# Rotary half-swaps by DMA, a third place for softmax weights, merged weight buffers, and another start, in a two-layer fp32 trunk on one core

## The chip, the core and the metric

The kernel runs on one core of a Trainium2 chip. The core has a matmul engine (TensorE, PE, with its weight loads listed as PEld), a vector engine (DVE), a scalar engine (ACT), a general engine (POOL) and an engine that only issues DMAs (SP). The metric is the device time of one execution in microseconds.

## The reference

Two layers over 512 positions of width 1024. Every layer does a mixer and a SwiGLU with width 2816, each between a pre-norm and a post-norm. The first mixer is sliding-window attention with 16 query heads, 4 key heads, rotary positions and a learned sink; the second is a gated unit that mixes positions in chunks of 128.

```python
for i in range(DEPTH):                       # 2
    h = rmsnorm(x, norm_mix_pre[i])
    m = swa_sink_attention(h, ...) if i % 2 == 0 else chunked_sgu(h, ...)
    x = x + rmsnorm(m, norm_mix_post[i])
    h = rmsnorm(x, norm_ffn_pre[i])
    x = x + rmsnorm(swiglu(h, ...), norm_ffn_post[i])

# rotary, in the attention, on q and k (after their bias)
x1, x2 = x[..., :half], x[..., half:]
concatenate([x1 * cos - x2 * sin, x2 * cos + x1 * sin])
# per head: window of 128 keys back, softmax with the sink in max and sum
m = maximum(max(s), sink); p = exp(s - m)
probs = p / (sum(p) + exp(sink - m)); o = probs @ v; out = o @ w_o + b_o
```

## The kernel before, in words

**Products.** Every fp32 product is done as three matmuls of a rounded type: high x high, high x low and low x high (`mm3`, line 272). The normed activations are kept as `hh` and `hl`, the weights as `wh` and `wl`. Weights stream from memory in chunks of 128 x 1024 (512 KB, tile `raw`), by DMAs on SP (`fetch`, L303). `split` makes `wh` on ACT (L344) and `wl` on DVE (L325), for the first two chunks on POOL (`POOL_LOW`, L322). The FFN's products need sums or differences of two chunks (L337). There are 4 buffers for `raw` and 15 of the same size for `wh`, `wl` and rows of gains.

**Order.** The order of the instructions on PE, DVE and ACT is written by the Python program itself: it keeps a planned time for each engine (`now`, `busy`), runs PE's work as the main thread, and lets side generators (`Side`, with a due time) put their DVE and ACT instructions in between. SP and POOL execute in the order in which the program issues; SP waits at an issue for a free buffer and for a free one of 8 rotating completion semaphores. Numbers such as `WARM`, `X_0` and `hold` are planned times, and so set where things stand and not how long they take.

**Start.** 26 matmuls on zeros (L240) run while x transposed (`xg`) and weights load; `c_cols` with the gains comes by a DMA on POOL. `start` makes `hh` on ACT (L1390) and `hl` on DVE (L1393). Then the V projection: 64 matmuls with `wh`, 32 with `wl`.

**Attention.** Ten tiles of the Q/K projection (2 groups of 1 key and 4 query tiles) run on PE, 24 matmuls each. `evac_qk` takes each out of PSUM: DVE multiplies with the norm's factor (L960); ACT copies four blocks of 32 partitions, each to its neighbour's place and with its bias, which is the half-swap of the rotary (L966); DVE does the three rotary operations (L969, L971, L972); ACT and DVE split the result in high and low (L976, L979; tiles `ga`, `gb`). Then eight softmax units (2 groups x 4 query blocks): scores on PE with mask and maximum on DVE (L1048), exponentials on ACT (L1070), division (L1079 on DVE, L1083 on ACT); transposes on PE (L1116), which ACT copies to `t` (L1120); P·V on PE (L1108); the output split on ACT (L1130) and DVE (L1135) into `ga`. A unit keeps its weights in one of two `p` tiles, so a unit's scores wait until the unit two before is done (`all_scores`). The output projection (WO) has 8 tiles of 12 matmuls per group, and DVE adds them into the tiles `m` (L1195, L1210); the second group's tiles go by token block (0 to 3, 128 positions each), two column halves each.

**Norms.** When a block's second half is added, the post-norm's chain of small DVE operations (L482 to L471) and the update of `x` (L617) follow. For blocks 0 and 1 together the next pre-norm comes next: another chain, a scaling (L514 or L523), transposes on PE (L552, L554), `hh` on ACT and `hl` on DVE (L571), for which the next product waits. The first FFN ends with blocks 0 and 1 interleaved matmul group by matmul group in both column halves, then block 2, then block 3 (L901).

Of the kernel before, what the change touches and what calls it, by code (L numbers as in the profile page):

```python
# [13 lines left out]
P = 128  # L14
D = 1024
S = 512
# [8 lines left out]
NW = 15  # L25
NP = 2
PITCH = 0.107
NY = 3
P0 = 3
NT = 3  # L30
NRAW = 4
# [7 lines left out]
X_0 = 4.0  # L39
# [5 lines left out]
POOL_LOW = (0, 1)  # L45
ALT = (1, 2, 3)
WARM = 5.5
ORDER = (0, "w", 1, 2, "w", 3)
# [101 lines left out]
def trunk_kernel(ctx, tc, x_t, xt, w, cols, rows, ws_t, consts, out):  # L150
# [7 lines left out]
    rawp = pool("rawp", NRAW)  # L158
# [127 lines left out]
    used, cur, hold, pace = [0], [0], [0.0], [5.1]  # L286
    left = [CB * u for _, _, u in STREAM]
    raw_used = [0]

    def fetch(free=0.0, most=NBLK):  # L290
        while len(raws) < min(NCH, most) and raw_used[0] + len(STREAM[len(raws)][0]) <= NRAW:
            c = len(raws)
            if c == NLATE:
                load_x()
# [6 lines left out]
            for b in reversed(STREAM[c][0]):  # L301
                raw = rawp.tile([P, CB * P], F32, tag="raw", name=nm("raw"))
# [6 lines left out]
    def split():  # L309
        c = len(chunks)  # L310
        fetch()
        tiles, ready = raws[c]
        raw = tiles[0]
        assert used[0] + 2 <= NW
# [34 lines left out]
    def split_idle():  # L349
        c = len(chunks)  # L350
        if c >= NCH or used[0] + 2 + spare[0] > NW or (c and not chunks[c - 1][2].done):
            return False
# [10 lines left out]
    spare, stage = [0], [0]  # L363

    def chunk(i):
        c = i // CB
        while c >= len(chunks):
            until(lambda: not chunks or chunks[len(chunks) - 1][2].done)
            split()
        return c, chunks[c]  # L370
# [19 lines left out]
    def row_tile(o):  # L390
        used[0] += 1
        assert used[0] <= NW
# [17 lines left out]
    c_cols = cp.tile([P, 42], F32, name="c_cols")  # L410
# [32 lines left out]
    def gain(v, k):  # L443
        return c_cols[:, v * KT + k:v * KT + k + 1]

# [258 lines left out]
    def ffn(base, nx_in, g1o, nx_out):  # L704
# [188 lines left out]
        if 1:  # L893
            spare[0] = 0
# [41 lines left out]
    def attention(nx_in, g1o, nx_out):  # L936
# [6 lines left out]
        ready = {}  # L943

        def evac_qk(pr, j, ps, hf):
# [10 lines left out]
            def rest(f):  # L956
# [7 lines left out]
                for q in range(4):  # L964
                    o = (q ^ 1) * 32
                    nc.scalar.activation(ro[o:o + 32, hf], t1[q * 32:q * 32 + 32, hf], AF.Identity, bias=b[q * 32:q * 32 + 32])  # L966
                    f = A(n, f, 0.14)
# [3 lines left out]
                nc.vector.tensor_tensor(ro[:, hf], ro[:, hf], sin[:, hf], ALU.mult)  # L971
# [10 lines left out]
                for t in range(hf.start // P, hf.stop // P):  # L982
                    ready[pr, j, t] = f

# [39 lines left out]
        def scores(u):  # L1024
# [6 lines left out]
            pt = u.pt = ptile()[:].rearrange("p g (i k) -> p g i k", i=2)  # L1031
            for g2 in range(2):
# [12 lines left out]
                for g in range(2):  # L1045
                    for i in range(2):
                        j = (2 * g2 + g) * 2 + i
                        nc.vector.tensor_tensor_reduce(  # L1048
                            pt[:, 2 * g2 + g, i, 0:nk], sc[i][:, g * 256:g * 256 + nk], mask[:, 256 - nk:256], 0.125,
# [12 lines left out]
        def softmax(u, g2, st, es, sm, f):  # L1062
# [3 lines left out]
            p = lambda j: u.pt[:, j // 2, j % 2, 0:u.nk]  # L1066
# [20 lines left out]
        def values(u):  # L1087
# [25 lines left out]
            for z, (i, kt) in enumerate(groups):  # L1113
                pT = aux()
                for g in range(4):
                    nc.tensor.transpose(pT[:, g * P:(g + 1) * P], u.pt[:, g, i, kt * P:(kt + 1) * P], ident)  # L1116
# [35 lines left out]

        def all_scores():
            for i, u in enumerate(order):
                while i >= NP and not order[i - NP].done:
# [3 lines left out]
        def all_values():  # L1159
            for u in order:  # L1160
                yield from values(u)
                u.done = True

# [19 lines left out]
        m = new_m()  # L1183
        stage[0] = 1
        bo = row_tile(3)
        for c, t in ([(c, t) for c in range(2) for t in range(NB)],
# [3 lines left out]
            if 1:  # L1190
                grab("acc")
                ps = acc()
                for k in range(4):
                    tok_mm(ps, osrc(0), t, k, WO0 + 16 * c + 4 * k, k == 0, k == 3)
                nc.vector.tensor_tensor(m[t][c][:], ps[:], bo[:, cols2[c]], ALU.add)  # L1195
# [255 lines left out]
def _layout(inputs):  # L1451
# [58 lines left out]
    vecs += [a["attn_b_qkv"][0][order]]  # L1510
# [36 lines left out]
```

## Time and profile before

| | us |
|---|---|
| median of 3 runs (1058.65 to 1059.26) | 1058.82 |
| the profiled execution | 1059.33 |
| its span | 1057.5 |
| PE busy | 1031.1 (97%) |
| DVE busy | 684.7 (65%) |
| ACT busy | 469.6 (44%) |
| start of the Q/K projection | 23.67 |
| start of the first FFN | 191.43 |
| second FFN's matmuls end near | 1049 |

The stages follow one another on PE: start and V to 23.7, Q/K to 88.8, softmax with WO to 191.4, first FFN to about 546, the gated unit, the second FFN to the end. In a row of the timeline stand start, duration, engine, line, operation, output and inputs, and in brackets the idle time before it with what ended it. A group's row has busy time, mean ns of one, and the idle time before. "Busy" of PE contains modelled ends of pipelined matmuls.

### The profile page before, as it was taken

How to read it: one execution, taken by the hardware profiler on the slowest of the kernel's cores; microseconds unless marked ns; L12 is line 12 of the kernel's file. 1: busy time of each engine (PE TensorE's matmuls, PEld its weight loads, DVE VectorE, ACT ScalarE, POOL GpSimd, SP SyncE). 2: the span in 40 equal slices, each digit the busy share in tenths (PEclk: the TensorE clock that was granted, in tenths of full speed). 3: DMA queues.
4: the chain of work that ended last, by engine and by line, in shares of the span. 5: the costliest groups of instructions: out<-in, count | busy, mean ns of one | idle time of the engine just before them, and what ended most of it. 6: DMA issues, size and time to landing. Idle time of an engine off the chain costs nothing.

```text
span 1057.5 us, 13471 instructions
## 1 busy us (share of the span) xinstructions
PE 1031.1 (97%) x5126; PEld 854.7 (81%) x5126; DVE 684.7 (65%) x1276; ACT 469.6 (44%) x817; POOL 23.8 (2%) x22
## 2 busy tenths in 40 slices
PE   8998998999999999999989999999999999999996
PEld 7875665998888888888878888899888888888885
DVE  6798678743446566778495777474245666687736
ACT  5798666542233343435265343464224333334411
POOL 2000002000000000000010000010000000000000
PEclk9998999999999999999999999999999999999999
DMA  9422011343425644655431333133344553565402
GB/s 334 138 82 80 21 60 41 100 127 113 139 82 178 199 122 157 222 188 191 156 116 60 104 103 121 56 121 120 120 140 131 178 174 124 188 203 193 163 21 80
DMA packets 39057, 138.66 MB, mean 131 GB/s; under 512 B 4368, under 2 KB 4896, under 8 KB 38992
## 3 DMA queue, kind: packets, MB, share of 16 engines
q1 hardware_dynamic: 38304, 136.66, 39.3%
q8 instruction: 40, 0.66, 0.3%
q10 hardware_dynamic: 576, 0.92, 0.2%
q0 software_dynamic: 112, 0.23, 0.2%
q14 instruction: 25, 0.20, 0.1%
HBM read 135.69 MB, written 2.10 MB: 130 GB/s over the span
## 4 chain that ended last, share of the span: by engine, by line
PE 92%; DVE 3%; ACT 2%; issue 1%; DMA 0%; POOL 0%; DVEq 0%; ACTq 0%; POOLq 0%
PE acc L272 89%; PE acc L1108 1%; PE aux L1116 1%; PE aux L554 1%; ACT p L1070 1%; DMA c_cols<-cols 0%; ACT rt L966 0%; DVE wl L325 0%; DVE x L617 0%; DVE hl L1393 0%; ACT wh L344 0%; PE aux L552 0%; ACT t L1120 0%; DVE m L1210 0%; DVE rc L471 0%
## 5 line engine op out<-in xcount | busy, mean ns | idle before, releaser
L272 PE MATMUL acc<-hh,wh 128*128 128x512 f32 (+1 forms) x960 | 352.1, 367 | 0.0
L272 PE MATMUL acc<-hl,wh 128*128 128x512 f32 (+1 forms) x960 | 349.9, 364 | 0.0
L272 PE MATMUL acc<-hh,wl 128*128 128x512 f32 (+1 forms) x960 | 349.7, 364 | 0.0
L325 DVE TENSOR_TENSOR wl<-raw,wh 128x1024 fp32r<-128x1024 f32 x198 | 241.9, 1230 | 151.1 <-PE acc L272 78.2
L272 PEld LDWEIGHTS acc<-hh,wh 128*128 128x128 f32 x960 | 181.1, 189 | 29.4 <-issue 0.2
L272 PEld LDWEIGHTS acc<-hh,wl 128*128 128x128 f32 x960 | 181.1, 189 | 28.7
L272 PEld LDWEIGHTS acc<-hl,wh 128*128 128x128 f32 x960 | 181.1, 189 | 28.6 <-issue 0.2
L344 ACT ACTIVATE wh<-raw 128x1024 fp32r<-128x1024 f32 x160 | 165.6, 1052 | 55.0 <-PE acc L272 48.3
L272 PE MATMUL acc<-wh,rt 128*128 128x512 f32 x496 | 162.3, 389 | 0.0
L272 PE MATMUL acc<-wh,ga 128*128 128x512 f32 (+1 forms) x344 | 120.3, 399 | 3.6 <-DVE ga L1135 2.9
L272 PEld LDWEIGHTS acc<-wh,rt 128*128 128x128 f32 x496 | 93.1, 188 | 19.4
L272 PE MATMUL acc<-wl,rt 128*128 128x512 f32 x248 | 96.5, 389 | 0.0
L272 PEld LDWEIGHTS acc<-wh,ga 128*128 128x128 f32 x344 | 65.2, 191 | 21.1 <-DVE ga L1135 3.8
L853 DVE TENSOR_TENSOR m<-m,acc 128x512 f32<-128x512 f32 x80 | 51.8, 684 | 44.2 <-PE acc L272 33.0
L272 PE MATMUL acc<-wl,ga 128*128 128x512 f32 (+1 forms) x206 | 80.0, 388 | 0.0
L332 ACT ACTIVATE wh<-raw 128x1024 fp32r<-128x1024 f32 x40 | 42.3, 1059 | 71.0 <-DVE raw L337 71.0
L831 ACT ACTIVATE rt<-t 128x512 fp32r<-128x512 f32 x40 | 25.3, 633 | 87.1 <-DVE t L826 68.7
L740 ACT ACTIVATE t<-acc 128x512 f32<-128x512 f32 (+1 forms) x38 | 20.1, 529 | 95.0 <-PE acc L272 95.0
L272 PEld LDWEIGHTS acc<-wl,rt 128*128 128x128 f32 x248 | 46.6, 188 | 9.6
L337 DVE TENSOR_TENSOR raw<-raw,raw 128x1024 f32<-128x1024 f32 x40 | 48.8, 1219 | 0.0
L272 PEld LDWEIGHTS acc<-wl,ga 128*128 128x128 f32 x206 | 39.3, 191 | 6.6
L598 POOL TENSOR_TENSOR m<-m,row 128x512 f32<-128x512 f32 x12 | 16.8, 1407 | 1012.1 <-ACT acc L476 1012.1
(135 smaller groups left out, 990.5 us busy)
## 6 DMA issues: line engine op xcount, KB each, us to landing
raw<-w SPq DMA_DIRECT2D x240, 512.0 KB, 3.6
row<-rows SPq DMA_DIRECT2D x8, 512.0 KB, 5.2
xg<-xt SPq DMA_DIRECT2D x4, 512.0 KB, 7.1
x<-x_t SPq DMA_DIRECT2D x4, 512.0 KB, 11.9
out<-x SPq DMA_DIRECT2D x4, 256.0 KB, 2.1
out<-x ACTq DMA_DIRECT2D x3, 256.0 KB, 2.1
cs<-consts SPq DMA_DIRECT2D x1, 512.0 KB, 8.3
t<-ws_t SPq DMA_DIRECT2D x2, 256.0 KB, 5.9
```

The costliest lines, as they stand in the source:

```text
L272: nc.tensor.matmul(ps, a, b, start=start, stop=stop)
L325: nc.vector.tensor_tensor(wl[:], raw[:], wh[:].bitcast(F32), ALU.subtract)
L332: nc.scalar.activation(wh[:], raw[:], AF.Copy)
L337: nc.vector.tensor_tensor(raw[:], raw[:], tiles[1][:], op)
L344: nc.scalar.activation(wh[:], raw[:], AF.Copy)
L554: nc.tensor.transpose(dst, self.src[t][k // 4][:, (k % 4) * P:(k % 4 + 1) * P], ident)
L598: nc.gpsimd.tensor_tensor(self.m[c][:], self.m[c][:], self.g1[:, cols2[c]], ALU.mult)
L740: nc.scalar.activation(t1[:, hf], pg[:, hf], AF.Silu)
L831: nc.scalar.activation(hi, src, AF.Copy)
L853: nc.vector.tensor_tensor(d, d, ps[i][:], ALU.subtract if sign == "-" else ALU.add)
L1070: nc.scalar.activation(p(j), p(j), AF.Exp, bias=st[:, j:j + 1], accum_out=sm[:, j:j + 1])
L1108: nc.tensor.matmul(po[i * 64:i * 64 + 64, :], vt[n - nkt + 1 + kt][:, o:o + 64], todo[2 * kt + i], start=kt == 0, stop=kt == nkt - 1)
```

## The change

**Half-swaps.** The four ACT copies of a Q/K tile become four DMAs of 32 x 512 (64 KB) on SP, from one tile of a pair to the other. A DMA adds no bias, so ten columns with the swapped bias join `c_cols` (42 to 52) and DVE adds it in the instruction that multiplies with the sine. The planner counts `ROT` = 4.0 us for them.

**Places for softmax weights.** Beside the two `p` tiles a unit can take four `m` tiles, as long as no `m` is in use by WO, or two pairs of rotary tiles once all ten tiles are rotated. `m` tiles are now taken one by one as WO needs them. In the order that the program writes, the `m` place is never taken and the rotary place once, by unit 5 (counted from 0).

**Buffers.** `raw` comes out of the same 19 buffers as `wh` and `wl`; at most 2 are `raw`, 4 in the two stages that need pairs of chunks.

**Start.** Weights are issued before x transposed; `c_cols` comes on ACT's queue, with a first activation that has ACT's table loaded; both first `wl` go to DVE; 37 instead of 26 matmuls on zeros.

**FFN ends.** Block 0's second half is finished before block 1's begins.

```diff
-NW = 15
+NW = 19
+ROT = 4.0
-NRAW = 4
+NRAW = (2, 4)
-X_0 = 4.0
+X_0 = 4.9
-POOL_LOW = (0, 1)
+POOL_LOW = ()
-WARM = 5.5
-ORDER = (0, "w", 1, 2, "w", 3)
+WARM = 8.0
+ORDER = ("w", 0, 1, 2, "w", 3)
...
-                now[0] += 0.214 if now[0] < 4.0 else 0.107
+                now[0] += 0.214
...
-        while len(raws) < min(NCH, most) and raw_used[0] + len(STREAM[len(raws)][0]) <= NRAW:
+        while len(raws) < min(NCH, most):
             c = len(raws)
+            n = len(STREAM[c][0])
+            if raw_used[0] + n > NRAW[stage[0] in (2, 6)] or used[0] + raw_used[0] + n > NW:
+                return
...
-                raw = rawp.tile([P, CB * P], F32, tag="raw", name=nm("raw"))
+                raw = wp.tile([P, CB * P], F32, tag="w", name=nm("raw"))
...
+    nc.scalar.dma_start(c_cols[:], cols)
+    first_act = sp.tile([P, 8], F32, tag="first", name="first", bufs=1)
+    nc.vector.memset(first_act[:], 0.0)
+    nc.scalar.activation(first_act[:], first_act[:], AF.Copy)
     nc.gpsimd.dma_start(c_id[:], consts[:, 1280:1408])
-    nc.gpsimd.dma_start(c_cols[:], cols)
...
-            ends = [(0, 0), (0, 1), (1, 0), (1, 1)]
+            ends = [((0, 1), 0), ((0,), 1), ((1,), 1), ((2,), 0), ((2,), 1), ((3,), 0), ((3,), 1)]
...
-            ends = [((0, 1), 0), ((0, 1), 1)] + [((2 + i,), c) for i, c in ends]
...
-                    hold[0] = now[0] + 4 * BJ * 0.65
+                    hold[0] = now[0] + 5 * BJ * 0.65
...
                 for q in range(4):
                     o = (q ^ 1) * 32
-                    nc.scalar.activation(ro[o:o + 32, hf], t1[q * 32:q * 32 + 32, hf], AF.Identity, bias=b[q * 32:q * 32 + 32])
-                    f = A(n, f, 0.14)
+                    nc.sync.dma_start(ro[o:o + 32, hf], t1[q * 32:q * 32 + 32, hf])
+                f += ROT
...
-                nc.vector.tensor_tensor(ro[:, hf], ro[:, hf], sin[:, hf], ALU.mult)
+                nc.vector.scalar_tensor_tensor(ro[:, hf], ro[:, hf], b_rot(i), sin[:, hf], ALU.add, ALU.mult)
...
+        homes = {"p": NP, "m": 4, "rt": 0}
+        def home(u):
+            if homes["p"]:
+                homes["p"] -= 1
+                u.home = "p"
+            elif len(todo_m) == 8 and homes["m"] == 4:
+                homes["m"] = 0
+                u.home = "m"
+            elif len(rotated) == 10 and slots["rt"] >= 2:
+                slots["rt"] -= 2
+                u.home = "rt"
+            else:
+                return False
+            return True
+
         def all_scores():
             for i, u in enumerate(order):
-                while i >= NP and not order[i - NP].done:
+                while not home(u):
                     yield now[0] + 0.2
                 yield from scores(u)
```

**Three places of the order.** The first is the Q/K projection on ACT, the middle of its first tiles, as it was before (`rt` are the rotary tiles):

```order
L344 ACTIVATE wh_389<-raw_190 128x1024
L344 ACTIVATE wh_404<-raw_237 128x1024
L966 ACTIVATE rt_398<-rt_398,c_cols 32x512 x4
L344 ACTIVATE wh_420<-raw_274 128x1024
L344 ACTIVATE wh_450<-raw_374 128x1024
L976 ACTIVATE gb_119<-rt_398 128x512
L966 ACTIVATE rt_441<-rt_441,c_cols 32x512 x4
L344 ACTIVATE wh_492<-raw_396 128x1024
L976 ACTIVATE ga_117<-rt_441 128x512
L966 ACTIVATE rt_483<-rt_483,c_cols 32x512 x4
```

and SP's issues in the changed kernel over the same tiles:

```order
L307 DMA raw_377<-w 128x1024
L307 DMA raw_408<-w 128x1024
L307 DMA raw_431<-w 128x1024
L978 DMA rt_402<-rt_402 32x512 x4
L978 DMA rt_445<-rt_445 32x512 x4
L307 DMA raw_462<-w 128x1024
L307 DMA raw_482<-w 128x1024
L307 DMA raw_523<-w 128x1024
L978 DMA rt_493<-rt_493 32x512 x4
L307 DMA raw_536<-w 128x1024
L978 DMA rt_538<-rt_538 32x512 x4
L978 DMA rt_574<-rt_574 32x512 x3
```

The half-swaps leave ACT's order and stand between the weight loads on SP, where only loads stood; the third tile's swaps stand behind three loads.

The second is DVE near the end of the attention: the last output split (`ga`, with the accumulator of the last P·V), the adds of WO tiles (`m`) and the updates of `x`. Before:

```order
L617 SCALAR_TENSOR_TENSOR x_91<-m_1013,rc_1826,x_91 128x512
L617 SCALAR_TENSOR_TENSOR x_91<-m_1014,rc_1826,x_91 128x512
L325 TENSOR_TENSOR wl_1838<-raw_1276,wh_1837 128x1024
L1210 TENSOR_TENSOR m_1016<-acc_1804,m_1016 128x512
L1135 TENSOR_TENSOR ga_118<-acc_1782,ga_117 128x4x128
```

and now:

```order
L630 SCALAR_TENSOR_TENSOR x_87<-m_1046,rc_1792,x_87 128x512
L630 SCALAR_TENSOR_TENSOR x_87<-m_1263,rc_1792,x_87 128x512
L1254 TENSOR_TENSOR m_1209<-acc_1754,m_1209 128x512
L1155 TENSOR_TENSOR ga_118<-acc_1713,ga_117 128x4x128
L1254 TENSOR_TENSOR m_1345<-acc_1804,m_1345 128x512
L1254 TENSOR_TENSOR m_1449<-acc_1821,m_1449 128x512
L328 TENSOR_TENSOR wl_1835<-raw_1750,wh_1834 128x1024
```

The last split stood behind block 1's update of `x` (`x_91`) and now stands ahead of block 1's chain, with only block 0's update (`x_87`) before it; two WO tiles are added behind it in these rows and three more later, where two followed before.

The third is DVE at the end of the first FFN. Before:

```order
L901 TENSOR_TENSOR m_2822<-acc_4485,m_2822 128x512
L901 TENSOR_TENSOR m_2824<-acc_4486,m_2824 128x512
L604 TENSOR_TENSOR m_2822<-m_2822,row_4479 128x512
L604 TENSOR_TENSOR m_2824<-m_2824,row_4479 128x512
L901 TENSOR_TENSOR m_2823<-acc_4528,m_2823 128x512
L901 TENSOR_TENSOR m_2825<-acc_4529,m_2825 128x512
L604 TENSOR_TENSOR m_2823<-m_2823,row_4479 128x512
L604 TENSOR_TENSOR m_2825<-m_2825,row_4479 128x512
```

and now:

```order
L913 TENSOR_TENSOR m_2843<-acc_4497,m_2843 128x512
L913 TENSOR_TENSOR m_2845<-acc_4498,m_2845 128x512
L617 TENSOR_TENSOR m_2843<-m_2843,row_4491 128x512
L617 TENSOR_TENSOR m_2845<-m_2845,row_4491 128x512
L913 TENSOR_TENSOR m_2844<-acc_4538,m_2844 128x512
L617 TENSOR_TENSOR m_2844<-m_2844,row_4491 128x512
L495 SCALAR_TENSOR_TENSOR u_4574<-sq_4493 128x1
```

Both blocks' second halves were added and given their gains before block 0's chain began (`u`, in the row behind the last); now block 0's chain starts after its own, and block 1's second half comes later.

More of the change, by code (lines that the diff above doesn't have):

```diff
@@ L286, in trunk_kernel @@
     used, cur, hold, pace = [0], [0], [0.0], [5.1]
+    stage = [0]
     left = [CB * u for _, _, u in STREAM]
@@ L350, in split_idle @@
         c = len(chunks)
-        if c >= NCH or used[0] + 2 + spare[0] > NW or (c and not chunks[c - 1][2].done):
+        if c >= NCH or used[0] + raw_used[0] + 2 > NW or (c and not chunks[c - 1][2].done):
             return False
@@ L361, in split_idle, with room @@
         return True
-    spare, stage = [0], [0]
+    def room():
+        fetch()
+        return len(chunks) in raws and used[0] + raw_used[0] + 2 <= NW
     def chunk(i):
@@ L367, in chunk @@
         while c >= len(chunks):
-            until(lambda: not chunks or chunks[len(chunks) - 1][2].done)
-            split()
+            until(lambda: c < len(chunks) or (not chunks or chunks[len(chunks) - 1][2].done) and room())
+            if c >= len(chunks):
+                split()
         return c, chunks[c]
@@ L390, in row_tile @@
     def row_tile(o):
+        until(lambda: used[0] + raw_used[0] < NW)
         used[0] += 1
-        assert used[0] <= NW
         t = wp.tile([P, D], F32, tag="w", name=nm("row"))
@@ L409, in trunk_kernel @@
     xs = [xp.tile([P, D], F32, tag=f"x{k}", name=f"x{k}") for k in range(NB)]
-    c_cols = cp.tile([P, 42], F32, name="c_cols")
+    c_cols = cp.tile([P, 52], F32, name="c_cols")
     c_msk = cp.tile([P, 384], F32, name="c_msk")
@@ L444, in gain, with b_rot @@
         return c_cols[:, v * KT + k:v * KT + k + 1]
+    def b_rot(i):
+        return c_cols[:, 42 + i:43 + i]
     def b_qk(i):
@@ L943, in attention @@
         ready = {}
+        rotated, todo_m = [], list(range(8))
         def evac_qk(pr, j, ps, hf):
@@ L1030, in scores @@
             st, es, sm = small(8, "st"), small(8, "es"), small(8, "sm")
-            pt = u.pt = ptile()[:].rearrange("p g (i k) -> p g i k", i=2)
+            if u.home == "m":
+                ms = [mp.tile([P, S], F32, tag="m", name=nm("pm"))[:] for _ in range(4)]
+            elif u.home == "rt":
+                ms = [x for _ in range(2) for x in pair()]
+            else:
+                t = ptile()
+                ms = [t[:, g] for g in range(4)]
+            u.pt = [t.rearrange("p (i k) -> p i k", i=2) for t in ms]
             for g2 in range(2):
@@ L1115, in values @@
                 for g in range(4):
-                    nc.tensor.transpose(pT[:, g * P:(g + 1) * P], u.pt[:, g, i, kt * P:(kt + 1) * P], ident)
+                    nc.tensor.transpose(pT[:, g * P:(g + 1) * P], u.pt[g][:, i, kt * P:(kt + 1) * P], ident)
                     now[0] += 0.11
@@ L1181, in attention @@
                 evac_qk(pr, j, proj_tile((Q0, Q1)[pr] + j * KT, KT, h, full), full)
-        m = new_m()
+        m = [[None, None] for _ in range(NB)]
         stage[0] = 1
@@ L1194, in attention @@
                     tok_mm(ps, osrc(0), t, k, WO0 + 16 * c + 4 * k, k == 0, k == 3)
+                until(lambda: homes["m"] + 3 >= 8 - len(todo_m) + 1 or homes["m"] == 4 and len(rotated) == 10)
+                todo_m.pop()
+                m[t][c] = mp.tile([P, S], F32, tag="m", name=nm("m"))
                 nc.vector.tensor_tensor(m[t][c][:], ps[:], bo[:, cols2[c]], ALU.add)
```

18 lines of the change are left out of this document (11 added, 7 removed).

## The prediction

> **What bounds the kernel now.** I read the shares of the engines first, then what the tensor engine (PE) waited for, then the windows by stage.
>
> ```profile
> PE 1031.1 (97%) x5126; PEld 854.7 (81%) x5126; DVE 684.7 (65%) x1276; ACT 469.6 (44%) x817; POOL 23.8 (2%) x22
> ```
> ```profile
> PE acc L1108 <- ACT t L1120: 6.6, 3, 3.8
> PE acc L272 <- ACT wh L344: 3.1, 1, 3.1
> PE acc L272 <- DVE ga L1135: 2.9, 2, 2.6
> PE acc L272 <- DVE hl L571: 2.7, 1, 2.7
> ```
>
> PE is busy 97% of the span and its work does not change, so a gain can only come from places where PE stands or runs at a reduced clock. The waits (us in total, times, longest) are four: the start (`wh` L344), the softmax (`t` L1120, `ga` L1135), and the norm behind the first FFN (`hl` L571). The windows show the stages around the attention; their columns are PE, PEld, DVE, ACT and POOL busy, granted clock, DMA share, GB/s.
>
> ```profile
> 55.00:88.80 33.80, 33.80 (x196) 26.23 (x195) 32.88 (x106) 32.56 (x84) 0.00 (x0) 1.00 0.29 95
> 88.80:107.80 19.00, 14.94 (x67) 7.99 (x66) 14.38 (x35) 15.17 (x33) 0.00 (x0) 0.82 0.17 55
> 107.80:146.00 38.20, 38.20 (x228) 27.42 (x227) 27.80 (x113) 23.14 (x77) 0.00 (x0) 1.00 0.13 42
> 146.00:191.40 45.40, 38.64 (x183) 25.65 (x182) 34.94 (x108) 28.12 (x76) 5.36 (x4) 0.92 0.15 47
> ```
>
> The Q/K projection ends near 88.8 and the first FFN begins near 191.4. Between them PE idles 4.1 us in the second row and 6.8 us in the fourth, and the clock falls there too. How much is lost in all I get from counts and paces. The first list holds PE's matmuls of 88.8 to 191.4, the second pieces of the chain of waits (start, duration, line, count) in which PE never stopped:
>
> ```profile
> L272 PE MATMUL acc<-wh,ga 128*128 128x512 f32 x128 | 48.3, 425 | 3.6 <-DVE ga L1135 2.9 <-ACT ga L1130 0.7
> L272 PE MATMUL acc<-wl,ga 128*128 128x512 f32 x64 | 26.0, 406 | 0.0
> L1108 PE MATMUL acc<-t,vt 128*64 128x512 f32 x52 | 19.1, 636 | 6.6 <-ACT t L1120 6.6
> L1116 PE MATMUL aux<-c_id,p 128*128 128x128 f32 x94 | 15.8, 298 | 0.5 <-ACT t L1120 0.5
> L272 PE MATMUL acc<-gb,ga 64*128 64x256 f32 x96 | 9.2, 331 | 0.0
> L552 PE MATMUL aux<-rt,x 128*128 128x128 f32 x16 | 2.1, 275 | 0.0
> L272 PE MATMUL acc<-gb,ga 64*128 64x128 f32 x24 | 1.8, 281 | 0.0
> ```
> ```profile
> 519.78 17.24 PE acc L272 x76
> 122.63 1.01 PE acc L1108 x4
> 106.91 0.91 PE acc L272 x12
> 188.62 0.89 PE aux L552 x8
> ```
>
> The paces are 17.24/76 = 0.227 us for a 512-wide matmul, 1.01/4 = 0.25 for P·V, 0.91/12 = 0.076 for a score matmul and 0.89/8 = 0.11 for a transpose. The work is 192 x 0.227 + 52 x 0.25 + 120 x 0.076 + 110 x 0.11 = 43.6 + 13.0 + 9.1 + 12.1 = 77.8 us of 102.6. So **24.8 us are lost**, and by the windows nearly all of it before 107.8 and after 146; split as idle plus lost clock stand there (7.5 against 10.4) that is about 10 and 14.
>
> **The start: gain 3.4.**
>
> ```profile
> 7.20 1.33 ACT L1390 ACTIVATE hh<-xg,c_cols 128x512 fp32r<-128x512 f32 x2 [1.07 <-DMA c_cols<-cols]
> 11.84 1.04 ACT L344 ACTIVATE wh<-raw 128x1024 fp32r<-128x1024 f32 x1
> 9.53 0.58 PE L272 MATMUL acc<-wh,hh 128*128 128x256 f32 x1 [3.08 <-ACT wh L344]
> 9.50:12.70 3.20, 3.17 (x15) 3.17 (x16) 2.57 (x2) 3.20 (x5) 2.37 (x1) 0.50 1.02 419
> 16.01 0.39 PE L272 MATMUL acc<-wh,hl 128*128 128x256 f32 x1 [0.84 <-DVE hl L1393]
> 13.07 2.89 DVE hl L1393
> 22.23 1.60 PE L272 MATMUL acc<-wl,hh 128*128 128x256 f32 x12
> 23.67 0.40 PE L272 MATMUL acc<-hh,wh 128*128 128x512 f32 x1
> ```
>
> PE idles 3.08 us before its first real matmul at 9.53, then runs at clock 0.50, then waits 0.84 us for an `hl` that took 2.89 us on DVE while POOL wrote a `wl`. The 12 `wl` matmuls from 22.23 to 23.67 pace at 0.12. Now weights land first, the constants come on ACT's queue, the warm matmuls (37 instead of 26) last until the real ones, and both `wl` are DVE's. What then ends last is the second weight chunk: it is fifth in the queue as before, and its `wh` ended by 12.9 (third number: 11.84 + 1.04). Behind it stand 32 matmuls with `wh` and 32 with `wl`: 64 x 0.12 = 7.7, so Q/K starts near 20.3 instead of 23.67. Bounds: 96 matmuls at 0.12 from an unimproved 9.53 end at 21.1, and with clock 0.50 for 3.2 us at 22.7, so 1.0 at least; 4.5 if the chunk lands 1 us sooner. I take 3.4, the row's own landing.
>
> **The Q/K projection: nothing, and the way into softmax: gain 2.**
>
> ```profile
> L966 ACT ACTIVATE rt<-rt,c_cols 32x512 f32<-32x512 f32 x32 | 23.1, 721 | 3.4 <-DVE rt L960 3.0
> out<-x SPq DMA_DIRECT2D x4, 256.0 KB, 2.1
> 10.46 0.33 SPq L303 DMA_DIRECT2D raw<-w  x1
> ```
>
> The first row is from the list of 27 to 88.8; the other 8 of the 40 half-swaps run after it. The change takes 40 ACT operations of 721 ns (28.8 us) away and adds 40 DMAs of 64 KB on SP, whose rows here are a store with its time from issue to landing and one issue. DVE keeps its operations (the bias moves into an instruction that is there already) and was busy 32.88 of 33.80 us from 55 to 88.8, against 32.56 for ACT: with ACT relieved, DVE still sets the pace, so I cost this edit at nothing in that stage. A tile's four halves took 4 x 0.72 = 2.9 us on ACT. The swap DMA is in no row; the nearest is the 256 KB store, 2.1 us from issue to landing, and with three earlier issues of 0.33 us the fourth lands after some 3.1 us (an estimate from these two rows). That is level with ACT; DVE has other tiles' work to fill it. From below, the swaps cost nothing; from above, each lands behind two weight loads, which the rivals price. After 88.8, PE's longest wait for `t`, 3.8 us, ended while ACT, busy 15.17 of 19.0 us, worked through those last eight halves (8 x 0.72 = 5.8 us) between the exponentials. Not all of that comes back: the last two tiles' DVE operations stay, and so do the exponentials, which the next unit's transposes wait for. I take 2 of the 10 us, a third of the 5.8, with bounds of 0 (DVE ends last there too) and 5.8.
>
> **From there to the FFN: gain 6.** Weights of unit 5 go to two idle rotary tiles; the `m` place is never taken in the written order. With ACT free, the last P·V now stands five WO tiles before the norm instead of before the last two. Then the wait for `ga` (2.6 us) goes, because that split is no longer queued on DVE behind the chains of blocks 0 and 1, and the wait for `t` in this stage (6.6 - 3.8 = 2.8, or less) should go, because the exponentials before it no longer share ACT with late work. But a new wait follows. Its durations are in these DVE rows of the first FFN's end:
>
> ```profile
> 537.65 1.32 DVE L482 SCALAR_TENSOR_TENSOR u<-s 128x1 f32<-128x1 f32 x2
> 539.98 0.23 DVE L471 SCALAR_TENSOR_TENSOR rc<-vw,vz 128x1 f32<-128x1 f32 x2
> 547.47 1.41 DVE L617 SCALAR_TENSOR_TENSOR x<-m,rc,x 128x512 f32<-128x512 f32 x2
> 548.80 0.68 DVE L901 TENSOR_TENSOR m<-acc,m 128x512 f32<-128x512 f32 x1
> 549.40 1.21 DVE L325 TENSOR_TENSOR wl<-raw,wh 128x1024 fp32r<-128x1024 f32 x1
> 550.54 0.87 DVE L571 SCALAR_TENSOR_TENSOR hl<-aux,c_cols,hh 128x256 fp32r<-128x256 f32 x2
> ```
>
> Once token block 1's last WO tile is added, DVE has four more adds (2.7), two `wl` (2.4), block 1's own chain with its `x` (1.2 + 1.4), the joint norm (539.98 + 0.23 - 537.65 = 2.6), its scaling (estimate 0.4) and block 2's chain and `x` (2.6) before the first `hl` (0.4): 13.7, and about one more where it waits for ACT's squares. PE has four WO tiles for it (48 x 0.227 = 10.9) and eight transposes (0.9). So PE stands about 3 us, runs on at half clock for some 3 us (lost: 1.7), and waits some 2 more for the fourth pair of `hl`, which stands behind block 3's chain. That makes 7 of new loss, with 1 in the middle, where 14 were lost: gain 6. Bounds: 12 if the walk's losses shrink to 2, and 0 if the softmax chain of the last units still ends as late.
>
> What the clock does after such a gap is read from two windows:
>
> ```profile
> 153.00:156.00 3.00, 3.00 (x18) 2.68 (x19) 1.89 (x8) 0.97 (x2) 0.00 (x0) 0.50 0.52 171
> 552.00:555.00 3.00, 3.00 (x10) 2.33 (x9) 3.00 (x6) 1.78 (x3) 0.00 (x0) 0.52 0.85 270
> ```
>
> They follow the softmax's second wait for `t` (6.6 - 3.8 = 2.8 us at most) and the 2.7 us wait for `hl`. The Trainium skill ("TensorE: Matmul & The Clock Gate", "HAM oscillation") rules that only idle gaps over about 3.4 us are to be avoided. By that rule a gap of 3 us would cost no clock and this part would gain 1.7 more; the rows show the clock at half after 2.8 and 2.7, so the trace does not agree, and I keep the 1.7.
>
> **The end of the first FFN: gain 4.** PE's 2.7 us wait for `hl` (L571) and the 0.52 clock behind it (0.48 x 3 = 1.4) are 4.1. Block 0's second half is now finished one tile (18 matmuls, 4.1 us) before block 1's, so the joint norm no longer has both chains behind each other ahead of it, and block 1's is one tile further from the transposes. Bounds: 0, if `hl` still stands behind block 2's chain, and 4.5. The second FFN's end keeps its chain; extra raw buffers meet no wait in the trace there: nothing.
>
> **Sum.** 3.4 + 2 + 6 + 4 = 15.4. The profiled execution took 1059.33 (span 1057.5 and 1.8 around it), so 1043.9 by it; the median of the runs before is 0.5 lower. I predict **1044**, with 1034 to 1054 for this case alone.
>
> **Rivals.**
> (1) The attention gains nothing: DVE was as full as ACT, and the relieved engine was never the one that ended last. For it: 32.88 of 33.80. Against it: after 146 DVE has a quarter idle. Only 3.4 and 4 stay: 1052.
> (2) Slower: the swaps come late. SP issues in order; a swap behind a weight load that waits for a free buffer stands with it, and in three of ten tiles the four swaps are split by such loads. What waits behind a late swap on DVE is the next tile's reading of its accumulator, and PE waits for that accumulator; DVE has 0.9 us idle in 33.8, so a late swap lengthens the projection almost directly. At 3 us for each of ten tiles it costs 30, of which I let a third be hidden behind other work; the attention's gains are lost with it: 1059.3 - 7.4 + 20 = 1072. It decides from 2.3 us a tile on, where 10 x 2.3 x 2/3 eats the 15.4. Against it: DMA share is 0.29 in that window. The Trainium skill ("DMA: Bandwidth & Descriptors", "Rules for kernel authors") says that small transfers under 64 KB are mostly overhead and that transfers on disjoint partition parts serialize; by it four in a row would take longer than one after the other issued, which is this rival's side. No row here shows four small transfers together.
> (3) The gap ahead of the norm stays too short to cost the clock, and the softmax chains close up: 1.7 of clock and about 4 of the 8 us that I left on the way into softmax are not lost, 1044 - 5.7 = 1038. This is also where the rule on the clock above leads. For it: ACT is free between the projection and the exponentials. Against it: the two clock rows, and DVE's unchanged work.
> (4) The third place itself does nothing, being used once; this is inside (1) and inside my 6, not priced again.
>
> **Chances.** Forecast 0.58; (1) 0.19; (2) 0.12; (3) 0.11. A measurement of this kernel tells 0.2% (2.1 us) from no change. Of (1), a third may end within it, if the start or the FFN end fails as well. Faster 0.58 + 0.11 + 0.13 = 0.82, same 0.06, slower 0.12. The range leaves out (2) and the low tail of (3): 1033 to 1058.
>
> **What would show it.** Right: first real matmul before 9, Q/K from about 20; no ACT half-swaps, DVE without waits over 1 us for `rt` before 88; last P·V more than 10 us before the FFN; a PE wait for `hl` of 2 to 4 us there; none near the first FFN's end. Wrong: DVE idle behind swap DMAs, PE waiting on `wh` in the projection, or the waits of `t` and `ga` of the same length as before.

## The result, and the profile after

The change takes 1045.34 us (median; 1044.23 to 1047.61) against 1059.04 (1058.65 to 1059.56) on the same chip: ratio 0.9873, 95% interval 0.9855 to 0.9891. The profiled execution took 1044.61 us, its span is 1042.8.

The engines' line, and PE's list of waits, of the changed kernel:

```profile
PE 1023.1 (98%) x5137; PEld 849.0 (81%) x5137; DVE 682.5 (65%) x1279; ACT 442.6 (42%) x778; POOL 19.0 (2%) x19
```
```profile
PE aux L565 <- DVE rt L527: 3.0, 1, 3.0
PE acc L272 <- DVE hl L584: 2.8, 2, 1.5
PE aux L1136 <- ACT p L1103: 2.3, 3, 1.6
PE acc L1128 <- ACT t L1140: 1.8, 1, 1.8
PE acc L240 <- DVE first L427: 1.1, 1, 1.1
```

The old list had `t` 6.6, `wh` 3.1, `ga` 2.9 and `hl` 2.7. The waits for `wh` and `ga` are gone or small, `t` is a third of what it was, and on top now stand two new ones of the norm ahead of the first FFN (`rt`, `hl`). The wait for `p` (2.3) is new too. ACT has 39 operations less: 40 half-swaps are DMAs, and one first activation was added.

Where the 14.7 us of span were gained is read from three marks: the first Q/K matmul, the first accumulation in the first FFN, the first 256-wide matmul of the gated unit. The timeline's rows of the changed kernel, then those of the kernel before that the prediction doesn't show:

```profile
6.87 0.36 PE L272 MATMUL acc<-wh,hh 128*128 128x256 f32 x1
20.45 0.40 PE L272 MATMUL acc<-hh,wh 128*128 128x512 f32 x1
104.81 0.48 PE L272 MATMUL acc<-wh,ga 128*128 128x512 f32 x1
307.01 1.36 DVE L866 TENSOR_TENSOR m<-m,acc 128x512 f32<-128x512 f32 x2
548.73 0.28 PE L272 MATMUL acc<-hh,wh 128*128 128x256 f32 x1
```
```profile
108.16 0.47 PE L272 MATMUL acc<-wh,ga 128*128 128x512 f32 x1
316.04 1.36 DVE L853 TENSOR_TENSOR m<-m,acc 128x512 f32<-128x512 f32 x2
562.50 0.28 PE L272 MATMUL acc<-hh,wh 128*128 128x256 f32 x1
```

The start gives 23.67 - 20.45 = 3.2; from Q/K to the first FFN 292.4 became 286.6, so 5.8; the end of the first FFN gives 246.5 - 241.7 = 4.7. The last 0.9 come in small steps behind. The middle part can be cut once more, at the rows of 108.16 and 104.81: a WO matmul that has the same softmax units and the same WO work ahead of it in both orders. There the lead is 3.35, hardly more than the start's 3.2, so nearly all of the 5.8 came later.

The gaps of PE in the timeline show what stands there now:

```profile
76.10 0.44 PE L1136 MATMUL aux<-c_id,p 128*128 128x128 f32 x2 [1.60 <-ACT p L1103]
87.67 0.73 PE L272 MATMUL acc<-wh,ga 128*128 128x512 f32 x2 [0.60 <-DVE ga L1155]
96.73 1.71 PE L1128 MATMUL acc<-t,vt 128*64 128x512 f32 x2 [1.77 <-ACT t L1140]
158.41 1.08 PE L1128 MATMUL acc<-t,vt 128*64 128x512 f32 x4
177.02 2.05 PE L565 MATMUL aux<-rt,x 128*128 128x128 f32 x16 [3.02 <-DVE rt L527]
180.83 0.39 PE L272 MATMUL acc<-hl,wh 128*128 128x256 f32 x1 [1.51 <-DVE hl L584]
188.50 0.39 PE L272 MATMUL acc<-hl,wh 128*128 128x256 f32 x1 [1.32 <-DVE hl L584]
```

The last P·V stands at 158.41, 18.6 us before the norm's transposes. From there on PE has WO alone, and then stands where the prediction put it: 3.02 before the transposes, 1.51 and 1.32 for pairs of `hl`. Near the first FFN's end no gap is left.

The swaps are not late, but not free of waits either. The DMA row has size and time from issue to landing; the second row is DVE's wait for them between 15 and 90 us:

```profile
rt<-rt SPq DMA_DIRECT2D x40, 64.0 KB, 2.0
```
```profile
DVE rt L981 <- DMA rt<-rt: 3.4, 4, 1.2
```

DVE waited 3.4 us for them in all, 1.2 at most. In the kernel before, the group of the same operation (its last field is the wait) stood as long for ACT, so one wait has taken the other's place:

```profile
L969 DVE SCALAR_TENSOR_TENSOR rt<-rt,c_cols,cs 128x512 f32<-128x512 f32 x8 | 6.0, 747 | 3.9 <-ACT rt L966 3.9
```

### The profile page after: what moved, and what is told of

It reads as the page before. It is cut to its first block, busy times and chain, and to the rows that moved or that the text cites. A ratio compares the mean times of both kernels' runs of the same rounds, so it can differ in the third digit from the quotient of the medians.

```text
span 1042.8 us, 13539 instructions
## 1 busy us (share of the span) xinstructions
PE 1023.1 (98%) x5137; PEld 849.0 (81%) x5137; DVE 682.5 (65%) x1279; ACT 442.6 (42%) x778; POOL 19.0 (2%) x19
## 4 chain that ended last, share of the span: by engine, by line
PE 91%; DVE 4%; DMA 2%; ACT 1%; SPq 1%; issue 1%; DVEq 0%; ACTq 0%
PE acc L272 88%; DMA rt<-rt 1%; PE aux L1136 1%; PE acc L1128 1%; PE aux L567 1%; DMA xg<-xt 1%; DVE wl L328 1%; DVE p L1068 1%; SPq L978 0%; DVE rt L981 0%; DVE rt L983 0%; DVE x L630 0%; DVE rt L984 0%; DVE vt L471 0%; ACT p L1090 0%
```

## The experiments

Each run is compared by its ratio to the kernel before on the same chip. The last three columns come from the profiled execution: the first mark, and the distances from there to the second and from that to the third.

| run | us | ratio (95%) | Q/K begins | to first FFN | to gated unit |
|---|---|---|---|---|---|
| before | 1059.0 | 1 | 23.7 | 292.4 | 246.5 |
| changed | 1045.3 | 0.9873 (0.9855-0.9891) | 20.5 | 286.6 | 241.7 |
| e1_swaps_act | 1045.2 | 0.9873 (0.9856-0.9889) | 20.6 | 287.0 | 241.7 |
| e2_two_places | 1044.9 | 0.9867 (0.9850-0.9883) | 20.4 | 286.7 | 241.7 |
| e3_old_start | 1047.3 | 0.9890 (0.9876-0.9905) | 23.7 | 285.9 | 241.7 |
| e4_old_ends | 1051.8 | 0.9935 (0.9916-0.9953) | 20.5 | 288.6 | 244.9 |
| e5_neither | 1044.6 | 0.9865 (0.9852-0.9879) | 20.9 | 286.2 | 241.7 |
| e8_start_ends_only | 1048.8 | 0.9907 (0.9893-0.9920) | 20.5 | 291.8 | 242.1 |
| e14_raw4 | 1049.4 | 0.9914 (0.9900-0.9927) | 20.5 | 291.8 | 242.1 |
| e11_buffers_only | 1049.9 | 0.9913 (0.9900-0.9927) | 23.7 | 282.9 | 246.4 |
| e12_split_buffers | 1047.0 | 0.9890 (0.9876-0.9903) | 20.8 | 288.2 | 242.2 |
| e7_no_pool_attn | 1046.4 | 0.9880 (0.9866-0.9893) | 20.5 | 286.2 | 241.7 |
| e10_late_nopool | 1042.0 | 0.9845 (0.9831-0.9858) | 20.5 | 283.8 | 241.7 |
| e15_two_late_nopool | 1044.6 | 0.9872 (0.9855-0.9888) | 20.8 | 284.9 | 241.7 |

### One part taken back at a time

**The swaps on ACT again:**

```diff
-                    nc.sync.dma_start(ro[o:o + 32, hf], t1[q * 32:q * 32 + 32, hf])
-                f += ROT
+                    nc.scalar.activation(ro[o:o + 32, hf], t1[q * 32:q * 32 + 32, hf], AF.Identity, bias=b[q * 32:q * 32 + 32])
+                    f = A(n, f, 0.14)
...
```

> The changed kernel with the half-swaps back on ACT (four copies with the bias, 721 ns each, no DMA); places, buffers, start and FFN ends stay changed. Theory A: the projection is paced by DVE (32.88 of 33.80 us busy), so giving ACT its 28.8 us back costs little; the last P.V still stands six WO tiles before the norm, because the third place set that: 1044 to 1048. Rival B: the relief of ACT carries the attention's gain of 5.7 us: 1050 to 1052, with PE waits for t (L1140) as long as in the kernel before (3.8 and 2.6 us). Rival C: the DMAs cost something that ACT's copies did not: under 1044.

Measured: 1045.15, as with the DMAs. In the profile the wait for `t` on the way into softmax is 3.1 us again at 96.96, with a second of 1.4 at 102.84, and the one of 1.6 at 76 is gone. So the DMAs relieve ACT where the prediction said, but what PE gains at 97 it loses at 76. The whole carries nothing that can be measured.

**Two places for softmax weights:**

```diff
-            elif len(todo_m) == 8 and homes["m"] == 4:
+            elif False:
...
-            elif len(rotated) == 10 and slots["rt"] >= 2:
+            elif False:
```

> The changed kernel with the two p tiles as the only places for softmax weights; the swaps stay DMAs. The last P.V then stands two WO tiles before the norm again. Theory A: the one use of the third place is what ends the softmax chain early; without it the waits for t and ga near the end come back (about 5 us with the clock): 1049 to 1052. Rival B: the place is used once and carries nothing, the freed ACT does: 1044 to 1046.

Measured: 1044.9. The third place carries nothing either. Nor did the run above show a need of the freed ACT, which is the rival's reason. Here PE has no wait of the norm at all, but one of 2.66 for `ga` at 174.2, where the changed kernel has 3.02 + 1.51 + 1.32: the place trades one wait for others.

**The old start** (order of the first loads, warm matmuls, `c_cols` on POOL's queue, `wl` on POOL):

```diff
-ORDER = ("w", 0, 1, 2, "w", 3)
+ORDER = (0, "w", 1, 2, "w", 3)
...
-POOL_LOW = ()
+POOL_LOW = (0, 1)
...
```

> The changed kernel with the start of the kernel before (x transposed first, c_cols by POOL's DMA, POOL makes two wl, 26 warm matmuls). The Q/K projection began 3.2 us earlier in the change. Theory A: all of it reaches the end: 1048 to 1049.5, projection from 23.7. Rival B: later stages wait for weights or the softmax in any case and take part of it back: under 1047.

Measured: 1047.3. Q/K begins 3.3 us later, but the loss is 2.0 us by the medians (2.7 in the profiled execution; the intervals overlap). With the other planned times the program writes another order, and the attention becomes 0.7 us shorter.

**The old FFN ends:**

```diff
-            ends = [((0, 1), 0), ((0,), 1), ((1,), 1), ((2,), 0), ((2,), 1), ((3,), 0), ((3,), 1)]
+            ends = [(0, 0), (0, 1), (1, 0), (1, 1)]
...
+            ends = [((0, 1), 0), ((0, 1), 1)] + [((2 + i,), c) for i, c in ends]
...
```

> The changed kernel with the FFN ends of the kernel before (blocks 0 and 1 interleaved in both halves). Theory A: the wait for hl of 2.7 us and the half clock behind it come back: 1049.5 to 1050.5, a PE idle of 2.5 to 3 us near 539. Rival B: the wait comes from DVE's other work there and has moved with it: within 2 us of 1045.

Measured: 1051.8, 6.5 us more; the profiled execution took 6.2 more. The wait for `hl` of 2.67 is back at 544.08, and the stretch behind the first FFN's first accumulation is 3.2 us longer. The half clock that the theory expected behind it is not back: the clock was 1.00 from 544 to 554 here, against the 0.52 of the kernel before.

Another 2.0 were lost ahead of that stretch, in a part that the edit does not touch. Near 100 us a transpose waited 1.70 for its `p` here and 0.17 in the changed kernel:

```profile
100.27 0.87 PE L1137 MATMUL aux<-c_id,p 128*128 128x128 f32 x6 [1.70 <-ACT p L1104]
```
```profile
100.77 0.88 PE L1136 MATMUL aux<-c_id,p 128*128 128x128 f32 x6 [0.17 <-ACT p L1103]
```

Behind the longer wait the clock was 0.85 (100 to 103) and 0.58 (103 to 106), and the norm's transposes start 1.1 us later than in the changed kernel (178.09 against 177.02). The last 1.0 lies behind the norm's gap, which cost clock in this execution and not in that of the changed kernel (below). About 1 us lies behind the gated unit's mark; I did not take it apart.

So each of the two named parts can go without loss, and still the attention is 5.8 us shorter than before. Either they stand in for each other, or something else carries it.

### Both parts taken back, and what then is left

Both edits above, of swaps and places, in one kernel:

```diff
-                    nc.sync.dma_start(ro[o:o + 32, hf], t1[q * 32:q * 32 + 32, hf])
+                    nc.scalar.activation(ro[o:o + 32, hf], t1[q * 32:q * 32 + 32, hf], AF.Identity, bias=b[q * 32:q * 32 + 32])
...
-            elif len(rotated) == 10 and slots["rt"] >= 2:
+            elif False:
...
```

> The changed kernel with both of its named parts taken back: the half-swaps are on ACT again and the softmax weights use two places. What stays is the new start, the new FFN ends, the merged weight buffers and the planner's order that follows from these. Theory R (the swaps and the third place stand in for each other, either suffices): the attention's 5.7 us are lost, so 1045.3 + 5.7 = 1051, with a wait for t over 3 us near the last units and waits for ga over 2.5. Theory O (neither carries it; the other order, the buffers or the start do): 1045 to 1046, the first accumulation of the first FFN at 307 to 308 as in the changed kernel.

Measured: 1044.55. Neither is needed. What is left beside the start and the ends are the shared weight buffers. The kernel before with start and ends alone (against the kernel before):

```diff
-ORDER = (0, "w", 1, 2, "w", 3)
+ORDER = ("w", 0, 1, 2, "w", 3)
...
-            ends = [(0, 0), (0, 1), (1, 0), (1, 1)]
+            ends = [((0, 1), 0), ((0,), 1), ((1,), 1), ((2,), 0), ((2,), 1), ((3,), 0), ((3,), 1)]
...
```

> The kernel before with only the new start and the new FFN ends: no merged weight buffers, no swap DMAs, two places. Theory B (the merged buffers give the order its freedom in the attention): only the start's 3.2 and the FFN end's 4.8 are there, and some 0.7 behind, 1059.0 - 8 to 9 = 1050 to 1051, with the before's waits for t (6.6 in all) and ga (2.9) still in the list. Theory O (any new order suffices): 1045 to 1047, first accumulation of the first FFN near 307 to 308.

Measured: 1048.8, somewhat under the first theory's range, and in the attention almost nothing is gained (291.8 against 292.4). The waits are not quite those of the kernel before: `t` has 3.8 and `ga` 5.0 in all. The shared buffers give 0.9907 - 0.9865 = 0.0042, or 4.4 us.

They differ from the old ones in two ways: `raw` comes from one pool with the split weights, and at most 2 of the 19 are `raw` in the attention (before, 4), so that 17 and not 15 can hold split weights. One number tells the shared pool from the new shares, in the kernel without the named parts:

```diff
-NRAW = (2, 4)
+NRAW = (4, 4)
```

> The run with neither named part (shared weight buffers, new start and ends, half-swaps on ACT, two places), with one number changed: up to 4 raw buffers in every stage, as before, so that in the attention 15 of the 19 shared buffers are left for split weights, and not 17. Theory room (the two more places for split weights let the program place its work otherwise in the second half of the attention): 1048 to 1049.5, as the kernel with the start and the ends alone, a wait for t of about 2.6 near 146 and one for ga near 179. Theory share (that the buffers are one pool is what counts): 1044.5 as the run with neither part.

Measured: 1049.4, with the waits of the kernel with start and ends alone. The pool as such does nothing; the **two places that pass from `raw` to split weights** do it (ratio 0.9914 against 0.9865, with intervals well apart). PE's waits with 15 places and with 17, then the windows of both (PE, PEld, DVE, ACT, POOL, clock, DMA share, GB/s):

```profile
PE acc L272 <- DVE ga L1155: 5.0, 3, 2.6
PE acc L1128 <- ACT t L1140: 3.8, 3, 2.6
```
```profile
PE acc L1128 <- ACT t L1140: 3.9, 1, 3.9
PE acc L272 <- DVE ga L1155: 3.8, 2, 2.7
```
```profile
146.00:180.00 34.00, 29.28 (x134) 18.65 (x135) 25.08 (x71) 20.60 (x55) 4.83 (x4) 0.90 0.05 16
180.00:200.00 20.00, 20.00 (x141) 18.87 (x140) 19.16 (x59) 12.50 (x27) 0.54 (x1) 0.91 0.36 119
```
```profile
146.00:180.00 34.00, 31.09 (x156) 21.10 (x157) 30.00 (x95) 22.46 (x59) 5.46 (x4) 0.95 0.12 41
180.00:200.00 20.00, 20.00 (x164) 19.69 (x163) 16.67 (x50) 13.84 (x29) 0.00 (x0) 1.00 0.32 117
```

The totals hardly differ, but the places do. With 15, a gap of 2.58 stands at 146.53 and one of 2.59 at 179.06, with the clock down behind both (0.90, 0.91). With 17 the longest, 3.9, is on the way into softmax, the one near 146 is gone, and DVE's work is brought forward: 30.00 against 25.08 us before 180, 16.67 against 19.16 behind. PE's rows around that spot show what fills it. With 15:

```profile
141.29 1.08 PE L1128 MATMUL acc<-t,vt 128*64 128x512 f32 x4
142.30 0.66 PE L1136 MATMUL aux<-c_id,p 128*128 128x128 f32 x4
142.88 1.07 PE L1128 MATMUL acc<-t,vt 128*64 128x512 f32 x2
146.53 1.97 PE L1128 MATMUL acc<-t,vt 128*64 128x512 f32 x2 [2.58 <-ACT t L1140]
```

and with 17:

```profile
142.88 1.08 PE L1128 MATMUL acc<-t,vt 128*64 128x512 f32 x4
143.89 0.50 PE L272 MATMUL acc<-wh,ga 128*128 128x512 f32 x1
144.22 0.39 PE L272 MATMUL acc<-wl,ga 128*128 128x512 f32 x1
144.45 0.39 PE L272 MATMUL acc<-wh,ga 128*128 128x512 f32 x1
144.69 0.60 PE L1136 MATMUL aux<-c_id,p 128*128 128x128 f32 x4
145.04 0.47 PE L272 MATMUL acc<-wh,ga 128*128 128x512 f32 x1
```

With 17, WO matmuls stand between this unit's products while PE would wait for its `t`. How the planner comes from the two places to this order I did not trace. That the number is the cause is shown, since it is the only edit. But it moves two limits at once: 17 instead of 15 places for split weights, and 2 instead of 4 chunks loaded ahead as `raw`. No run moves one without the other. That the room counts, and not the fewer chunks ahead, is argued from the trace: the 19th `wl` of the kernel starts at 119.8 us with 17 places and at 132.5 with 15, and the 21st to 24th some 5 us earlier, though the 20th 4 us later.

**The buffers alone**, in the kernel before:

```diff
-NW = 15
+NW = 19
-NRAW = 4
+NRAW = (2, 4)
...
-                raw = rawp.tile([P, CB * P], F32, tag="raw", name=nm("raw"))
+                raw = wp.tile([P, CB * P], F32, tag="w", name=nm("raw"))
...
```

> The kernel before with only the shared weight buffers (19, at most 2 raw in the attention): old start, old FFN ends, half-swaps on ACT, two places. Theory room: the attention's gain alone, 1059 - 4.5 to 5.5 = 1053.5 to 1054.5, no wait for t over 2 us after 140. Theory together (the room gives its gain only with the new start's or ends' order): within 1 us of 1059.

Measured: 1049.9. That is 9.2 us by the ratio, nearly twice what was expected: the attention falls to 282.9, the shortest of all runs. With the new start and the same buffers it is 286.2 (both parts taken back). So the gains of the start and of the buffers don't add up: at the first FFN's mark the kernel with the new start and ends is 3.8 us ahead, this one 9.4, and both parts together 8.9. What is lost lies on the way into softmax. With the new start PE stands there for 1.18 and 3.95 us and then has a clock of 0.57 and 0.75 for 5 us each (95 to 105); here it stands for 0.91 and 2.39 and has 0.66 for 5 us. By the clock's share of the time that is some 8.5 us against 5.0, about the 3.3 between 286.2 and 282.9. How much of it is the chance of the clock in one execution (below), these two traces don't tell.

**The changed kernel without the shared buffers** (the same lines the other way round, 15 and 4 apart):

```diff
-NW = 19
+NW = 15
...
-NRAW = (2, 4)
+NRAW = 4
...
```

> The changed kernel with the weight buffers as before (15 for split weights, 4 for raw); half-swaps by DMA, third places, new start and ends stay. Theory room: the attention loses its gain, 1048.5 to 1051. Theory either (room, or the named parts, each give the attention's gain alone): 1043 to 1046, with the last P.V early before the norm as in the changed kernel and the norm's wait for hl of 2 to 4 us.

Measured: 1047.0, between the two theories. With start and ends everywhere, the four corners are

| | 15 places | 17 places |
|---|---|---|
| neither named part | 1048.8, 1049.4 | 1044.6 |
| both | 1047.0 | 1045.3 |

The named parts give about 2.5 us where room is short (0.9890 against 0.9914 of the same chip, with intervals that just overlap) and none where it is not. The room gives 4.4 us without them; with them, 1.7 us that the intervals don't tell from nothing.

### The norm's new wait

The prediction made the norm's wait out of block 2's and 3's chains on DVE. Some small operations of the chains ahead of the norm took over 1 us in the profile, each time while POOL was at a gain operation (`m` times a row). First the changed kernel, then the run with that operation on DVE:

```profile
169.09 1.03 DVE L471 SCALAR_TENSOR_TENSOR vt<-vy,u 128x1 f32<-128x1 f32 x1
174.57 1.26 POOL L611 TENSOR_TENSOR m<-m,row 128x512 f32<-128x512 f32 x1 [4.48 <-ACT acc L489]
174.85 1.13 DVE L471 SCALAR_TENSOR_TENSOR vt<-vy,u 128x1 f32<-128x1 f32 x2
```
```profile
167.36 0.22 DVE L471 SCALAR_TENSOR_TENSOR vt<-vy,u 128x1 f32<-128x1 f32 x1
172.94 0.35 DVE L471 SCALAR_TENSOR_TENSOR vt<-vy,u 128x1 f32<-128x1 f32 x2
```

The edit is the last field of the attention's entry in the planner's table, the token blocks whose gains POOL takes:

```diff
-(6.0, 0.8, 0.0, (3,), (1, 2))
+(6.0, 0.8, 0.0, (3,), ())
```

> The changed kernel with the gains of the first norm (m times a row, on POOL in the attention stage) on VectorE instead. Theory P (a POOL operation that runs beside them makes VectorE's small operations about 1 us longer, which is part of the norm's stall): the 0.2 to 0.3 us operations of the post chains are no longer over 1 us there; VectorE takes on 4 more operations of about 0.7 us, and the stall of 3.0 us ahead of the transposes becomes 1 to 2.5, so 1043 to 1045. Theory N (the length is the operations' own): they stay over 1 us, the stall grows by the 2 to 3 us of added work, 1047 to 1048.

The pair of `vt` falls from 1.13 to 0.35, so the length came from POOL. In time nothing is gained (1046.4; the intervals overlap): the wait ahead of the transposes falls from 3.02 to 0.90, and the next, for `hl`, grows from 1.51 to 3.83, because block 2's chain and its `x` stand before it on DVE as they did, and now two `wl` as well. To hold those chains back too:

```diff
+            self.late = stage[0] == 1 and t > 1
...
-            r, = rstd([self.s[:, 0:2]], ready)
+            while self.late and (1, KT - 1) not in self.nx.ready:
+                yield now[0] + 0.2
+            r, = rstd([self.s[:, 0:2]], max(ready, now[0]))
```

> As the run without POOL in the attention stage, and the post chains of token blocks 2 and 3 are held back until the hl of blocks 0 and 1 are ready. By the prediction's working the stall of the norm (3.0 + 1.5 + 1.3 us of waits and about 1.7 of clock) comes of block 2's and 3's chains that stand between the joint norm and hl on VectorE. If so, it shrinks to 1 to 3 us in all and the time is 1040 to 1042. If what ends last is block 1's own chain, the stall stays at 3 us and the time at 1044 to 1046.

Measured: 1042.0, ratio 0.9845. First the norm's waits without POOL, then with the chains held back as well:

```profile
PE acc L272 <- DVE hl L584: 3.8, 1, 3.8
PE aux L565 <- DVE rt L527: 0.9, 1, 0.9
```
```profile
PE acc L272 <- DVE hl L584: 1.3, 2, 0.8
PE aux L565 <- DVE rt L527: 0.9, 1, 0.9
```

In all, the norm's waits are 5.9 us in the changed kernel (3.02 + 1.51 + 1.32), 4.7 without POOL and 2.2 with the chains held back; the attention takes 283.8. Against the run without POOL, on the same chip, the intervals are apart (0.9831 to 0.9858, and 0.9866 to 0.9893). It is the fastest kernel of the study, some 3 us under the changed one, though there the ends of the two intervals touch (0.9858, 0.9855). So the larger part of the stall is what the prediction named, block 2's and 3's chains ahead of `hl`: take them away from there, and it goes. The rest that went, 1.1 us, came with POOL's work, which the prediction did not have.

With that cured, does the third place pay? The same kernel with two places:

```diff
...
-            elif len(rotated) == 10 and slots["rt"] >= 2:
+            elif False:
...
```

> The run with post chains of blocks 2 and 3 held back and no POOL in the attention stage (1042.0), with the softmax weights in two places only. Theory late gain (the third place moves the last P.V ahead, and that pays once the norm's stall behind it is taken away): without it the wait for ga of 2 to 3 us near 174 comes back and the time is 1043.5 to 1045. Theory nothing (the third place carries nothing here either): 1041.5 to 1042.5, because VectorE's chains ahead of that ga are about 2 us shorter without POOL and the wait is under 1 us.

Measured: 1044.6. Without the place, a wait for `ga` of 1.96 is there at 172.5, and the attention is 1.1 us longer. That is what the place's theory asked for, but the intervals overlap (0.9855 to 0.9888 against 0.9831 to 0.9858), so it stays likely, not shown.

## Why the prediction was right, and where it was not

The time (1044 against 1045.34) and three of the four terms were about right, but the largest term for another reason than the one given. That its size came out is luck, and so in part is the sum.

**Start, 3.4:** 3.2 measured at the mark, by the steps named: the first real matmul at 6.87, the second chunk's `wh` done at 12.6 (forecast 12.9), Q/K at 20.45. Its worth for the whole is less, 2.0 to 2.7 us, because the planner answers the earlier start with another order.

**Way into softmax, 2:** about 0.1 measured (3.35 - 3.2). The step that failed is "Not all of that comes back", which still let a third of the eight halves' time come back: the exponentials were left as they were, and the units start earlier and meet waits of their own, 1.60 at 76.1 and 0.57 at 89.7 for a `p`, 0.60 for `ga`. The wait for `t` did fall, from 3.78 to 1.77, as ACT was relieved.

**From there to the FFN, 6:** 5.7 measured (9.03 - 3.35), and the wait that was to replace the old ones stood in its place with 3.0 + 1.5 + 1.3. But the step that gave the cause failed: it was put into ACT's relief and the rotary place; the same gain is there without both, by the two places that pass from `raw` to split weights, which the prediction had only at the second FFN, at nothing. And two sizes were off and made up for each other. The 1.7 us of clock behind the new gap were not lost in the profiled execution, and nothing in the middle, so that 5.9 are lost and not the 8 of the forecast. The old loss was put at 14 by scaling up the 10.4 that the windows show; 5.7 gained and 5.9 left make it 11.6.

**End of the first FFN, 4:** 4.7 measured; the wait of 2.7 and the low clock behind it are gone. With the old order the wait comes back and 3.2 of the 4.7 with it; the low clock did not in that execution.

**The rivals.** That the attention gains nothing is refuted by the marks. But its mechanism is what the runs show: ACT's relief buys nothing that can be measured (1045.2 with the swaps back on ACT). Neither the forecast nor a rival had the gain in the buffers. That the swaps come late is refuted: 2.0 us from issue to landing, 3.4 us of DVE's waits in all. The Trainium skill ("DMA: Bandwidth & Descriptors", "Rules for kernel authors") has transfers under 64 KB as mostly overhead: the swaps stand just at that size, and the trace agrees in so far as a swap of 64 KB took 2.0 us and a store of 256 KB 2.1. Yet DVE's waits for four behind one another were no longer than for ACT's four (3.4 against 3.9 in all). Half of the third rival (no clock lost) came true in the profiled execution, and not in that of the run with the old FFN ends. That the third place does nothing was priced inside the others, and is what the runs show for the changed kernel.

## What to carry to other kernels

When several edits come together, take each back alone and then all at once: two parts that can each go without loss may still share the gain, and here a third one, the buffers, which I had priced at nothing, carried it. In a kernel whose order is written by a planner, the number of buffers is part of the order: two places passed from `raw` to split weights put matmuls where a gap had been, and gains of two edits didn't add (3.8 of the start and 9.4 of the buffers, each without the other, but 8.9 together, all at the first FFN's mark). Where an engine stands before a norm, look at what is queued on the vector engine between the last input and the norm's output, and hold back what is due later.

## What was not expected of the hardware

**The clock behind a gap.** The same gap of 3.02 us before the norm's transposes cost clock in one execution and none in another. First the windows of the changed kernel, then the gap's row and the windows of the one with the old FFN ends (the clock is the third number from the end):

```profile
174.00:177.00 3.00, 0.00 (x0) 0.00 (x0) 3.00 (x19) 1.11 (x4) 1.26 (x1) 1.00 0.88 313
177.00:180.00 3.00, 2.29 (x17) 2.05 (x17) 2.78 (x12) 2.21 (x7) 0.00 (x0) 1.00 0.66 259
```
```profile
178.09 2.29 PE L565 MATMUL aux<-rt,x 128*128 128x128 f32 x9 [3.02 <-DVE rt L527]
```
```profile
178.00:181.00 3.00, 2.91 (x13) 2.92 (x14) 2.78 (x13) 1.52 (x4) 0.00 (x0) 0.50 0.68 274
181.00:184.00 3.00, 3.00 (x16) 2.89 (x15) 2.46 (x6) 2.09 (x7) 0.00 (x0) 0.50 0.00 0
```

In the changed kernel a gap of 1.77 at 96.73 was followed by 0.50, with PE busy for only 1.23 of the 3 us before:

```profile
97.00:100.00 3.00, 3.00 (x15) 1.41 (x13) 2.90 (x8) 0.98 (x3) 0.00 (x0) 0.50 0.38 153
```

In the run with the old FFN ends the same gap of 1.77, at 96.22, was followed by 1.00 (97 to 100). And the wait of 2.7 for `hl` at the first FFN's end was followed by 0.52 in the kernel before and by 1.00 in the run with the old FFN ends. So a gap's length alone doesn't tell whether it costs clock.

Nor is the lost clock the time lost. Up to 102 us the run with the old ends keeps a lead of 0.5 us over the changed kernel, whether the clock behind the gap of 1.77 was 0.50 or 1.00, because PE then waits for the next `p` in any case: 0.17 after the half clock, 1.70 after the full one. And behind the norm's gap 6 us at about 0.50 cost that run only 1.0 us, since the wait of 1.51 for `hl` is gone there.

The five times of the kernel with start and ends alone spread with the clock, from 1047.54 at a mean clock of 0.996 to 1050.72 at 0.991. The Trainium skill ("TensorE: Matmul & The Clock Gate", "HAM oscillation") has gaps over some 3.4 us cost the clock. Here 1.77, 2.7 and 3.02 each did in one execution and not in another, so the trace doesn't agree with a bound on the length. For an estimate it is better to give such a gap both prices than one.

**POOL and DVE.** A 128x512 product on POOL made single DVE operations of 0.15 to 0.35 us last over 1 us, though they share no data. An operation with one input beside it kept its time (`vy` from `u`, at 168.90: 0.15 us). The Trainium skill ("SBUF — State Buffer", "SBUF: two separate sides") has the two engines share a pair of ports by an exclusive lock, held for the whole instruction, when the DVE one has two SBUF inputs and the POOL one reads SBUF; the 1.13 against 0.35 us, and their end with POOL's work gone, agree with it.
